# Strassen's method in the last feed-forward: seven block products in place of eight

## The chip, the cores and the metric

The kernel runs on one core of a Trainium2 chip. The metric is the device time of one execution in microseconds (us). It has five engines at work: TensorE multiplies matrices, ScalarE and VectorE do elementwise work and read TensorE's results from PSUM, GpSimd does elementwise work between tiles in SBUF, and SyncE (SP) issues the loads.

## The reference, cut to what matters

A two-layer backbone over 512 latent tokens (and 256 context tokens), width 1024, all in float32. Each layer has two feed-forwards around a token mixer. The last feed-forward of layer 1 works on the latents alone:

```python
def swiglu(h, w_in, w_out):
    gate, up = jnp.split(h @ w_in, 2, axis=-1)
    return (jax.nn.silu(gate) * up) @ w_out
...
x = x + 0.5 * m_lat[:, 8] * swiglu(modulate(rms_norm(x), m_lat[:, 6], m_lat[:, 7]), ffn_in[l, 1], ffn_out[l, 1])
...
return rms_norm(x, final_gain)
```

`w_in` is 1024 x 5632, `w_out` 2816 x 1024, so the two products take 512 x 1024 x 5632 and 512 x 2816 x 1024 multiplications.

## The kernel before

**Layout.** Activations lie feature-major: 8 tiles of 128 features x 512 tokens (`s.X`, `hs`). The 2816 hidden features are 22 row blocks of 128, worked in three parts of 8, 8 and 6 (`PARTS`, L30). A weight block of 128 x 128 is the stationary operand, 512 tokens are the moving one.

**Three matmuls for one product.** Every operand is split into a high part, rounded to fp32r, and the low rest: `split` (L114) makes the high part on ScalarE (L116) and the low part on VectorE (L117). `mm3` (L136) multiplies high by high, high by low and low by high (L138 to L140), all into one bank of PSUM.

**The stage.** `norm_mod` (L407) normalises the latents: for each of 8 feature tiles `modulate` writes x on VectorE (L403), the high part with the shift added on ScalarE (L404) and the low part on VectorE (L405). `ffn` (L422) then goes through a part's row blocks: for each one `weights` loads (L129) and splits four weight tiles of 128 x 512, and 2 x 8 x 3 matmuls fill one bank for gate and one for up. The gate takes a tanh on ScalarE (L466) and two VectorE operations with an operand in PSUM (L467, L468); the result is split into a `pL` tile. When a part is complete, each of the 8 output blocks is summed over the part's row blocks, and VectorE adds it, gated, to X (L487). In the last part ScalarE squares each new X block (L350), and GpSimd sums the squares (L354) for the final norm (`rms`, L356, then L1532).

**Order.** The stage has all 8 PSUM banks (`ps4`, pool d). The instruction order of each engine is laid out by the scheduler of the tile framework ahead of time; inside `merge` the order of TensorE is that of the program. Tiles with one tag share a fixed number of buffers, and a new one waits until the oldest is free: 4 raw weight tiles, 3 high and 3 low ones. The stage is called at the end of `run`, between the odd layer's output projection and the final norm.

Of the kernel before, what the change touches and what calls it, by code (L numbers as in the profile page):

```python
# [11 lines left out]
F32R = mybir.dt.float32r  # L12
I32 = mybir.dt.int32
AF = mybir.ActivationFunctionType
ALU = mybir.AluOpType
# [4 lines left out]
P = 128  # L20
D = 1024
KD = 8
NL = 512
# [5 lines left out]
NEG = -1e30  # L29
PARTS = ((0, 8), (8, 8), (16, 6))  # L30
LEVELS = (2, 4, 8, 16)


C_QG, C_KG, C_MU0, C_MU1 = 0, 1, 2, 17
# [8 lines left out]
def flat(x):  # L43
    return x.rearrange("p a t -> p (a t)")
# [26 lines left out]
class Kernel:  # L71
# [32 lines left out]
    def pair(self, s, tag, dtype=F32R):  # L104

        if tag == "hC":
            if not self.spare:
                x = self.t(self.ap, [P, 2, 2, s.T], tag, dtype)
                self.spare = [(x[:, i, 0], x[:, i, 1]) for i in (1, 0)]
            return self.spare.pop()  # L110
        x = self.t(self.ap, [P, 2, s.T], tag, dtype)
        return x[:, 0], x[:, 1]
# [32 lines left out]
    def go(self, gen):  # L145
        try:
            while True:
                next(gen)
        except StopIteration as e:
            return e.value  # L150
# [245 lines left out]
    def modulate(self, s, l, i, k, r, out):  # L396

        nc, m = self.nc, self.mods[l, s]
        shift, scale = m[:, i, k : k + 1], m[:, i + 1, k : k + 1]
        if k % 2 == 0:  # L400
            s.x = self.pair(s, s.g, F32)
        x = s.x[k % 2]
        nc.vector.scalar_tensor_tensor(x, s.X[k], scale, r, op0=ALU.mult, op1=ALU.mult)  # L403
        nc.scalar.activation(out[0], x, AF.Identity, bias=shift)  # L404
        nc.vector.scalar_tensor_tensor(out[1], x, shift, out[0].bitcast(F32), op0=ALU.add, op1=ALU.subtract)  # L405
# [16 lines left out]
    def ffn(self, l, f, streams, hs=None, bg=(0, 0), into=None):  # L422

        nc, aps = self.nc, self.aps
        i0 = 0 if f == 0 else 6
        start = hs is not None
        if hs is None:
            hs = {}
            for s in streams:
                hs[s] = yield from self.norm_mod(s, l, i0)  # L430
        win, wout = aps["ffn_in"][l, f], aps["ffn_out"][l, f]
        alone = len(streams) == 1
        ws = streams[0]
        for m0, part in PARTS:
            G = {s: [] for s in streams}
            for mi in range(part):
                pt = {}
                for s in streams:
                    if s is self.L:
                        pt[s] = (self.bank_of(s), self.bank_of(s))  # L440
                    else:
                        b = self.bank_of(s)
                        pt[s] = (b[:, :256], b[:, 256:])
                w = {}

                if streams == (self.L,):
                    order = [(g, k, streams) for k, g in itertools.product((0, 4), (0, 1))]
                elif start and not m0 + mi:
                    order = [(0, 0, streams), (1, 0, streams[:1]), (0, 4, streams), (1, 0, streams[1:]), (1, 4, streams)]
                else:  # L450
                    order = [(g, k, streams) for g, k in itertools.product((0, 1), (0, 4))]
                for g, k0, ss in order:
                    if ss[0] is ws:
                        w[g, k0] = self.weights(win[m0 + mi][:, g * 1024 + k0 * P :], 512, ws)
                    for k in range(k0, k0 + 4):
                        for s in ss:
                            while len(hs[s]) <= k:
                                yield None
                            self.mm3(pt[s][g], w[g, k0][k % 4], *hs[s][k], k == 0, k == KD - 1)
                        if k % 4 == 3 or k % 2 and alone:  # L460
                            self.background(bg[0])
                            yield sum(s.T for s in ss) / 400 * (1 if alone else 2), 0
                for s in streams:
                    pg, pu = pt[s]
                    a = self.t(self.fp, [P, NL], "fL", bufs=1 if s.lock else 2) if s is self.L else self.small("x", 4)
                    nc.scalar.activation(a, pg, AF.Tanh, scale=0.5)  # L466
                    nc.vector.scalar_tensor_tensor(a, a, 1.0, pg, op0=ALU.add, op1=ALU.mult)  # L467
                    nc.vector.tensor_tensor(a, a, pu, op=ALU.mult)  # L468
                    G[s].append(self.pair(s, s.g))
                    self.split(a, *G[s][mi])  # L470
                if alone:
                    yield from self.rest()
            last = m0 + part == NM

            for ss in [(s,) for s in streams[::-1]] if last else [streams]:
                X = {s: s.X for s in ss}
                if last and into and self.L in ss:
                    self.L.X = yield from into()
                for d in range(KD):
                    w = self.weights(wout[d][:, m0 * P : (m0 + part) * P], part * P, ws)  # L480
                    for s in ss:
                        po = self.bank_of(s)[:, : s.T]
                        for mi in range(part):
                            self.mm3(po, w[mi], *G[s][mi], mi == 0, mi == part - 1)
                        yield s.T * part / 800, 0
                        gate = self.mods[l, s][:, i0 + 2, d : d + 1]
                        nc.vector.scalar_tensor_tensor(s.X[d], po, gate, X[s][d], op0=ALU.mult, op1=ALU.add)  # L487
                        if last:
                            self.square(s, d, nc.gpsimd)
                    self.background(bg[1])  # L490
                    if alone:
                        yield from self.rest()
                if last:
                    ss[0].done.add((l, f))


    def project(self, src, hs, s, use, wait=False):
# [823 lines left out]
    def run(self):  # L1321
        nc, tc, aps, stop = self.nc, self.tc, self.aps, self.stop
        L, C, go = self.L, self.C, self.go
        with ExitStack() as ctx:
            def pool(n, **k):
                return tc.tile_pool(name=n, reuse_waits="tile", **k)
# [32 lines left out]
            with pool("ps", bufs=1, space=PSUM) as self.ps, pool("fp", bufs=1) as self.fp:  # L1359
# [18 lines left out]
                hs = {L: [], C: []}  # L1378
# [145 lines left out]
            with pool("ps4", bufs=1, space=PSUM) as self.ps, pool("fp3", bufs=1) as self.fp:  # L1524
                self.banks = dict(d=8)
                L.use(self.wp, self.tp, "d", acc)
                go(self.w_out(aps["odd_out"], L.o, L, 1, slice(4, 8)))
                go(self.ffn(1, 1, (L,)))
                r, _ = go(self.rms(L))
                for k in range(KD):  # L1530
                    x = L.X[k]
                    nc.vector.scalar_tensor_tensor(x, x, self.par[:, C_FG + k : C_FG + k + 1], r, op0=ALU.mult, op1=ALU.mult)  # L1532
                    nc.sync.dma_start(aps["out"][k * P : (k + 1) * P], x)
# [75 lines left out]
```

## Time and profile before

| what | us |
|---|---|
| median of three timed runs | 3230.58 (3228.81 to 3232.74) |
| the profiled execution | 3231.14 |
| its span, first to last instruction | 3229.4 |
| the stage's first matmul starts | 2852.41 |
| its last matmul starts | 3213.42 |
| mean granted TensorE clock | 0.981 |

The span is the time on which the profile's shares are based; the rest of the profiled execution lies around it. A row of the timeline gives start, duration, engine, line, operation, the tiles written and read, and shapes. Rows of one line can overlap, above all on TensorE, where the next matmul starts before the last one has drained; its cost in a dense stream is the distance between two starts. A row that ends in brackets tells how long the engine had been idle and what ended that.

### The profile page before, as it was taken

To read this page: it belongs to the slowest core of one execution; us is meant where nothing else is said; L and a number is where in the kernel's file an instruction comes from. 1 tells how busy PE (TensorE), PEld (TensorE's weight loads), DVE (VectorE), ACT (ScalarE), POOL (GpSimd) and SP (SyncE) were. 2 spreads that over 40 slices of the span, in tenths; PEclk is the share of its full clock that TensorE was granted. 3 is DMA by queue.
4 is the path that set the end of the run, shared out by engine and by line. 5 is a ranking of instruction groups with operands and counts; after the bars stand their busy time and mean duration, and the time that the engine had idled before them with its cause. 6 is when DMAs were issued, how large, how long until landed. Compare 5 with 4: busy or idle time off the path is not lost. (4 is left out here: it accounts for less than half of the span.)

```text
span 3229.4 us, 57800 instructions
## 1 busy us (share of the span) xinstructions
PE 3065.0 (95%) x22910; PEld 2619.3 (81%) x22910; DVE 2012.3 (62%) x3956; ACT 1246.7 (39%) x2595; POOL 309.8 (10%) x333
## 2 busy tenths in 40 slices
PE   5999999988999899998999999999999988999998
PEld 3888888886777788887888888888888877778887
DVE  7999983675667677777766434454444667744434
ACT  4222212444444444444444323343233556632322
POOL 3000000112232110102101000010000132010001
PEclk8999999999999899999999999999999999999999
DMA  6666671531112023332344333333333320023332
GB/s 225 208 212 216 215 259 59 167 105 49 43 46 80 23 87 98 97 97 71 99 141 138 105 97 96 96 116 98 95 98 93 110 74 24 27 83 97 98 97 87
DMA packets 174431, 349.59 MB, mean 108 GB/s; under 512 B 19408, under 2 KB 30544, under 8 KB 173776
## 3 DMA queue, kind: packets, MB, share of 16 engines
q1 hardware_dynamic: 169984, 340.86, 34.1%
q10 hardware_dynamic: 4176, 5.05, 0.5%
q8 instruction: 179, 2.93, 0.4%
q14 instruction: 92, 0.75, 0.1%
HBM read 340.59 MB, written 5.24 MB: 107 GB/s over the span
## 5 line engine op out<-in xcount | busy, mean ns | idle before, releaser
L116 ACT ACTIVATE whi<-raw 128x512 fp32r<-128x512 f32 (+1 forms) x996 | 615.5, 619 | 1364.5 <-PE d L139 498.6
L117 DVE TENSOR_TENSOR wlo<-raw,whi 128x512 fp32r<-128x512 f32 (+1 forms) x996 | 682.9, 688 | 685.4 <-ACT whi L116 671.9
L138 PE MATMUL d<-hL,whi 128*128 128x512 f32 x944 | 381.8, 405 | 3.9 <-ACT hL L404 3.9
L139 PE MATMUL d<-hL,whi 128*128 128x512 f32 x944 | 375.6, 398 | 1.8 <-DVE hL L405 1.8
L140 PE MATMUL d<-hL,wlo 128*128 128x512 f32 x944 | 373.2, 396 | 1.8 <-DVE wlo L117 1.8
L138 PE MATMUL d<-hC,whi 128*128 128x256 f32 x968 | 297.8, 308 | 7.4 <-ACT whi L116 4.3
L140 PE MATMUL d<-hC,wlo 128*128 128x256 f32 x968 | 278.1, 287 | 11.4 <-DVE wlo L117 11.4
L284 DVE SCALAR_TENSOR_TENSOR junk<-qL,cb 128x1024 bf16<-128x1024 f32 x224 | 273.4, 1221 | 12.2 <-DMA qL<-wmod 9.6
L139 PE MATMUL d<-hC,whi 128*128 128x256 f32 x968 | 276.9, 286 | 0.0
L140 PEld LDWEIGHTS d<-hL,wlo 128*128 128x128 f32 x944 | 180.4, 191 | 43.7 <-DVE wlo L117 3.1
L138 PEld LDWEIGHTS d<-hC,whi 128*128 128x128 f32 x968 | 188.1, 194 | 22.0 <-issue 7.5
L138 PEld LDWEIGHTS d<-hL,whi 128*128 128x128 f32 x944 | 180.8, 192 | 28.0 <-ACT hL L404 5.6
L139 PEld LDWEIGHTS d<-hL,whi 128*128 128x128 f32 x944 | 180.9, 192 | 23.8 <-DVE hL L405 3.1
L140 PEld LDWEIGHTS d<-hC,wlo 128*128 128x128 f32 x968 | 188.4, 195 | 14.0 <-DVE wlo L117 13.7
L139 PEld LDWEIGHTS d<-hC,whi 128*128 128x128 f32 x968 | 188.6, 195 | 0.5
L138 PE MATMUL d<-pL,whi 128*128 128x512 f32 x416 | 162.8, 391 | 0.0
L140 PE MATMUL d<-pL,wlo 128*128 128x512 f32 x416 | 162.2, 390 | 0.6 <-DVE wlo L117 0.6
L139 PE MATMUL d<-pL,whi 128*128 128x512 f32 x416 | 162.2, 390 | 0.0
L138 PE MATMUL g<-hL,whi 128*128 128x512 f32 x384 | 149.4, 389 | 0.0
L139 PE MATMUL g<-hL,whi 128*128 128x512 f32 x384 | 149.4, 389 | 0.0
L140 PE MATMUL g<-hL,wlo 128*128 128x512 f32 x384 | 149.4, 389 | 0.0
L354 POOL TENSOR_TENSOR acc<-acc,sq 128x512 f32<-128x512 f32 x30 | 38.9, 1297 | 925.9 <-issue 708.4
(533 smaller groups left out, 6596.5 us busy)
## 6 DMA issues: line engine op xcount, KB each, us to landing
raw<-ffn_in SPq DMA_DIRECT2D x528, 256.0 KB, 2.9
qL<-wmod SPq DMA_DIRECT2D x132, 512.0 KB, 4.2
raw<-ffn_out SPq DMA_DIRECT2D x248, 256.0 KB, 2.7
raw<-even_in SPq DMA_DIRECT2D x84, 256.0 KB, 2.6
raw<-even_out SPq DMA_DIRECT2D x32, 256.0 KB, 2.6
raw<-odd_in SPq DMA_DIRECT2D x32, 256.0 KB, 2.8
raw<-ffn_out SPq DMA_DIRECT2D x56, 128.0 KB, 2.1
pL<-wmod SPq DMA_DIRECT2D x8, 512.0 KB, 8.7
```

The lines of the kernel that those rows point to most:

```text
L116: self.nc.scalar.activation(hi, src, AF.Copy)
L117: (eng or self.nc.vector).tensor_tensor(lo, src, hi.bitcast(F32), op=ALU.subtract)
L138: mm(out, w[0], mh, start=first, stop=False)
L139: mm(out, w[0], ml, start=False, stop=False)
L140: mm(out, w[1], mh, start=False, stop=last)
L284: nc.vector.scalar_tensor_tensor(self.t(self.fp, [P, D], "junk", bf), w, 0.5, self.cb[:, v], op0=ALU.mult, op1=ALU.mult, accum_out=out)
L354: eng.tensor_tensor(s.sq[0], s.sq[0], x, op=ALU.add)
```

## The change

The last feed-forward is computed by `ffn7` in place of `ffn`. A product of 2 x 2 blocks is formed from seven products of block sums (Strassen's method in Winograd's form) and not from eight products. The 2 x 2 blocks are: for the weights, gate and up rows (or two output blocks) by the two halves of the features summed over; for the activations, the two halves of the features by the two halves of the tokens, so that each matmul has 256 moving columns.

- `forms` makes, from a pair of activation tiles, the four block sums T1 to T4 on GpSimd (256 columns each) and splits them, beside the blocks that are used as they are. For the normed input this is done four times, on `xs` (the x of `modulate`, to which ScalarE adds the shift in place); for the gated blocks, once for each pair of row blocks.
- `seven` loads four weight blocks, makes S1 to S4 on GpSimd, splits the seven left operands (the low part of S4 on GpSimd, the others on VectorE), runs the seven products into four PSUM banks, and combines them into `z` in SBUF: three VectorE sums that read PSUM, two ScalarE copies and one GpSimd sum.
- Row blocks 0 and 4 are still computed in the old way (`whole`), while the first `forms` run. The first row block of the next part is computed before the outputs of a part.

```diff
-                go(self.ffn(1, 1, (L,)))
+                self.merge(self.ffn7(1, 1))
@@ modulate
             s.x = self.pair(s, s.g, F32)
+            s.xs = s.xs if k else []
         x = s.x[k % 2]
+        s.xs.append(x)
@@
+SUMS, RAWS = 3, 1
...
+    def forms(self, b1, b2, tiles, plain=None):
+        nc = self.nc
+        if plain is None:
+            ba, bb = tiles[1:]
+            self.split(b1[:, :256], *ba)
+            self.split(b2, *bb)
+        else:
+            ba, bb = plain
+        a, b = slice(0, 256), slice(256, 512)
+        two = lambda x, c: (x[0][:, c], x[1][:, c])
+        F = dict(B11=two(ba, a), B21=two(bb, a), B22=two(bb, b))
+        t13, t24 = (self.t(self.tp, [P, 512], "sq", bufs=2) for _ in (0, 1))
+        tt = nc.gpsimd.tensor_tensor
+        tt(t13[:, a], b1[:, b], b1[:, a], op=ALU.subtract)
+        tt(t24[:, a], b2[:, b], t13[:, a], op=ALU.add)
+        tt(t13[:, b], b1[:, b], b2[:, b], op=ALU.add)
+        tt(t24[:, b], b2[:, a], t24[:, a], op=ALU.subtract)
+        parts = [("T1", t13[:, a]), ("T3", t13[:, b]), ("T2", t24[:, a]), ("T4", t24[:, b])]
+        whole = [t13, t24]
+        for x in tiles[0]:
+            if x[0].shape[1] == 512:
+                self.split(whole.pop(0), *x)
+                for c in (a, b):
+                    F[parts.pop(0)[0]] = two(x, c)
+            else:
+                name, y = parts.pop(0)
+                self.split(y, *x)
+                F[name] = x
+        return F
+    def seven(self, srcs, n, F, plain_first=False):
+        nc, K = self.nc, n // P
+        add, sub = ALU.add, ALU.subtract
+        w = {}
+        for name, src in zip(("A11", "A22", "A21", "A12"), srcs):
+            tag = next(self.raws)
+            x = w[name] = self.t(self.ap if tag == "aC" else self.fp, [P, 512], tag, bufs=RAWS)[:, :n]
+            nc.sync.dma_start(x, src)
+        for name, x, y in (("S3", "A21", "A11"), ("S1", "A21", "A22"), ("S2", "A22", "S3"), ("S4", "A12", "S2")):
+            w[name] = self.t(self.fp, [P, 512], "sum", bufs=SUMS)[:, :n]
+            nc.gpsimd.tensor_tensor(w[name], w[x], w[y], op=sub)
+        one, b57, b26, b34 = (self.bank() for _ in range(4))
+        two = lambda x: x.rearrange("p (a t) -> p a t", a=2)
+        out = dict(P1=one[:, :256], P5=b57[:, :256], P7=b57[:, 256:], P2=b26[:, :256], P6=b26[:, 256:], P3=b34[:, :256], P4=b34[:, 256:])
+        z = self.t(self.ap, [P, 4, 256], "xC")
+        order = [("P1", "A11", "B11"), ("P4", "A22", "T4"), ("P7", "S3", "T3"), ("P5", "S1", "T1"), ("P2", "A12", "B21"), ("P6", "S2", "T2"),
+                 ("P3", "S4", "B22")]
+        if plain_first:
+            order = [order[i] for i in (0, 4, 6, 5, 3, 2, 1)]
+        done = set()
+        for o, a, b in order:
+            tags = next(self.splits)
+            hi, lo = (self.t(self.wp, [P, 512], t, F32R, bufs=4 if t == "raw" else 3)[:, :n] for t in tags)
+            self.split(w[a], hi, lo, nc.gpsimd if a == "S4" else None)
+            for k in range(K):
+                c = slice(k * P, (k + 1) * P)
+                self.mm3(out[o], (hi[:, c], lo[:, c]), *F[k][b], not k, k == K - 1)
+            yield 0.35 * K
+            done.add(o)
+            if o == "P1":
+                p1 = self.small("sw", 2, self.tp)
+                nc.scalar.activation(p1, out[o], AF.Copy)
+            if o == "P5":
+                p5 = self.small("x", 4, self.tp)
+                nc.scalar.activation(p5, out[o], AF.Copy)
+            if o in ("P2", "P6") and done >= {"P2", "P6"}:
+                nc.vector.tensor_tensor(z[:, 0:4:3], two(b26), p1.unsqueeze(1).to_broadcast([P, 2, 256]), op=add)
+            if "u" not in done and done >= {"P2", "P6", "P5", "P7"}:
+                done.add("u")
+                u = self.t(self.fp, [P, 2, 256], "u", bufs=1)
+                nc.vector.tensor_tensor(u, two(b57), z[:, 3:4].to_broadcast([P, 2, 256]), op=add)
+                nc.gpsimd.tensor_tensor(z[:, 3], u[:, 1], p5, op=add)
+        nc.vector.tensor_tensor(z[:, 1:3], two(b34), u, op=add)
+        return z
+    def ffn7(self, l, f):
+        nc, aps, s = self.nc, self.aps, self.L
+        tt, stt = nc.vector.tensor_tensor, nc.vector.scalar_tensor_tensor
+        i0 = 0 if f == 0 else 6
+        hs = yield from self.norm_mod(s, l, i0)
+        xs = s.xs
+        win, wout = aps["ffn_in"][l, f], aps["ffn_out"][l, f]
+        both = lambda x: (x[:, 0], x[:, 1])
+        self.raws = itertools.cycle(["aC"] * 4 + ["A"] * RAWS)
+        self.splits = itertools.cycle([("whi", "wlo")] * 3 + [("raw", "raw")] * 2)
+        G = {}
+        def gated(g, u, mi, then):
+            a = self.t(self.fp, [P, NL], "fL", bufs=3)
+            nc.scalar.activation(a, g, AF.Tanh, scale=0.5)
+            stt(a, a, 1.0, g, op0=ALU.add, op1=ALU.mult)
+            tt(a, a, u, op=ALU.mult)
+            then(mi, a)
+        def whole(mi, then):
+            pg, pu = self.bank(), self.bank()
+            for k0, (g, pt) in itertools.product((0, 4), enumerate((pg, pu))):
+                w = self.weights(win[mi][:, g * 1024 + k0 * P :], 512, s)
+                for k in range(k0, k0 + 4):
+                    self.mm3(pt, w[k % 4], *hs[k], k == 0, k == KD - 1)
+                yield 2.7
+            gated(pg, pu, mi, then)
+        def chunk(m0, h):
+            def then(mi, a):
+                G[mi] = a
+                if mi >= m0 + h:
+                    pair = lambda: both(self.t(self.ap, [P, 2, 512], "pL", F32R))
+                    tiles = [[pair(), both(self.t(self.fp, [P, 2, 512], "t24", F32R, bufs=4))],
+                             both(self.t(self.fp, [P, 2, 256], "b11", F32R, bufs=4)), pair()]
+                    G[mi - h, mi] = self.forms(G.pop(mi - h), G.pop(mi), tiles)
+            return then
+        def inputs(m0, h, j):
+            mi = m0 + j // 2 + h * (j % 2)
+            z = yield from self.seven([win[mi][:, c : c + 512] for c in (0, 1536, 1024, 512)], 512, F)
+            z = flat(z)
+            gated(z[:, :512], z[:, 512:], mi, chunk(m0, h))
+        def outputs(m0, h, d, last):
+            srcs = [wout[d + i][:, (m0 + j * h) * P : (m0 + j * h + h) * P] for i, j in ((0, 0), (1, 1), (1, 0), (0, 1))]
+            z = yield from self.seven(srcs, h * P, [G[m0 + k, m0 + k + h] for k in range(h)], last and not d)
+            z = flat(z)
+            for i in (0, 1):
+                X = s.X[d + i]
+                stt(X, z[:, 512 * i : 512 * i + 512], self.mods[l, s][:, i0 + 2, d + i : d + i + 1], X, op0=ALU.mult, op1=ALU.add)
+                if last:
+                    self.square(s, d + i, nc.gpsimd)
+        m0, part = PARTS[0]
+        for mi in (0, part // 2):
+            yield from ((x, 0) for x in whole(mi, chunk(0, part // 2)))
+        F = []
+        for k in range(4):
+            for i in (k, k + 4):
+                nc.scalar.activation(xs[i], xs[i], AF.Identity, bias=self.mods[l, s][:, i0, i : i + 1])
+            tiles = [self.t(self.ap, [P, 2, n], tag, F32R) for tag, n in (("hC", 512), ("gC", 256), ("gC", 256))]
+            F.append(self.forms(xs[k], xs[k + 4], [[both(x) for x in tiles]], plain=(hs[k], hs[k + 4])))
+        todo = range(2, part)
+        for n, (m0, part) in enumerate(PARTS):
+            h, last = part // 2, n == len(PARTS) - 1
+            for j in todo:
+                yield from ((x, 0) for x in inputs(m0, h, j))
+            if not last:
+                m1, p1 = PARTS[n + 1]
+                yield from ((x, 0) for x in inputs(m1, p1 // 2, 0))
+                todo = range(1, p1)
+            for d in range(0, KD, 2):
+                yield from ((x, 0) for x in outputs(m0, h, d, last))
```

`split` takes the engine of the low part as its last argument; `mm3`, `bank` and `weights` are those of before.

## The prediction

> **What bounds the kernel now.** I read the page's busy shares first, then the windows over the stage that changes, then single matmuls.
>
> ```profile
> PE 3065.0 (95%) x22910; PEld 2619.3 (81%) x22910; DVE 2012.3 (62%) x3956; ACT 1246.7 (39%) x2595; POOL 309.8 (10%) x333
> ```
>
> PE is TensorE, DVE VectorE, ACT ScalarE, POOL GpSimd. TensorE is busy 95% of the 3229.4 us span. The stage in question is the last one. Columns of the windows: length, busy us and count of PE, weight loads, DVE, ACT, POOL, granted clock, DMA share, GB/s.
>
> ```profile
> 2873.00:2938.00 65.00, 65.00 (x288) 53.84 (x287) 27.94 (x42) 21.89 (x36) 0.00 (x0) 1.00 0.32 98
> 2938.00:2983.00 45.00, 45.00 (x200) 37.26 (x199) 17.57 (x26) 11.82 (x19) 0.00 (x0) 1.00 0.34 97
> ```
>
> The first is input products, the second output products. TensorE has no gap, VectorE is at 40%, ScalarE at 30%, GpSimd does nothing. So a cut in TensorE's work counts in full as long as the other engines keep up. What one matmul costs is read from starts, as the busy times overlap:
>
> ```profile
> 2900.17 0.39 PE L138 MATMUL d<-hL,whi 128*128 128x512 f32 x1
> ...
> 2901.98 0.39 PE L140 MATMUL d<-hL,wlo 128*128 128x512 f32 x1
> ```
> ```profile
> 1639.76 0.28 PE L140 MATMUL d<-gC,wlo 128*128 128x256 f32 x1
> ...
> 1641.20 0.28 PE L140 MATMUL d<-gC,wlo 128*128 128x256 f32 x1
> ```
>
> Eight steps lie between the first two starts: 0.2267 us for 512 columns. Twelve lie between the second two: 0.120 us for 256 columns, each with a weight load of its own.
>
> **What TensorE saves.** Before: 22 row blocks x 2 x 8 x 3 = 1056 input matmuls and 8 x 22 x 3 = 528 output matmuls, 1584 x 0.2267 = 359.0 us. After: two row blocks stay whole (96 x 0.2267 = 21.8). Twenty calls of `seven` make inputs, each 7 x 4 x 3 = 84 narrow matmuls (10.08 us, in place of 10.88). Twelve make outputs: eight of 84, four of 63 (7.56 us). That is 2604 x 0.120 = 312.5, with the whole ones 334.3. **TensorE alone saves 24.7 us.** Weights are loaded in the same number of bytes (four 256 KB loads per row block or pair of outputs, as now), so the SP queue gets no more work.
>
> **What the others must now do.** Durations:
>
> ```profile
> L117 DVE TENSOR_TENSOR wlo<-raw,whi 128x512 fp32r<-128x512 f32 x119 | 82.0, 689 | 131.7 <-ACT whi L116 131.7
> L116 ACT ACTIVATE whi<-raw 128x512 fp32r<-128x512 f32 x119 | 75.2, 632 | 212.6 <-PE d L139 210.3 <-PE d L140 2.4
> L468 DVE TENSOR_TENSOR fL<-fL,d 128x512 f32<-128x512 f32 x21 | 14.4, 687 | 21.2 <-PE d L140 21.2
> L466 ACT ACTIVATE fL<-d 128x512 f32<-128x512 f32 x21 | 12.2, 579 | 0.0
> L354 POOL TENSOR_TENSOR acc<-acc,sq 128x512 f32<-128x512 f32 x6 | 7.8, 1294 | 356.2 <-issue 342.2 <-ACT sq L350 14.0
> L116 ACT ACTIVATE whi<-raw 128x256 fp32r<-128x256 f32 x8 | 3.3, 418 | 9.7 <-PE d L139 9.7
> ```
>
> One `seven` for a row block needs, per 10.08 us of TensorE:
> - ScalarE: 7 splits x 0.63, copies of P1 and P5 (2 x 0.42), a tanh 0.58, half of the four splits in `forms` (1.16): 7.0 us. Covered.
> - VectorE: 6 splits x 0.69, three sums from PSUM x 0.69, two gate products x 0.69, half of `forms` (1.25): 8.8 us.
> - GpSimd: four sums of weight blocks and the low part of S4, 5 x 1.29, one 256-wide sum and half of four 256-wide ones in `forms` (0.74 each, next rows): 8.7 us.
>
> If these ran side by side, all would lie under TensorE. The trace shows that they don't:
>
> ```profile
> 2543.83 0.68 DVE L117 TENSOR_TENSOR wlo<-raw,whi 128x512 fp32r<-128x512 f32 x1
> 2544.43 0.47 DVE L403 SCALAR_TENSOR_TENSOR gC<-xC,mod1C,d 128x256 f32<-128x256 f32 x1
> 2544.82 1.13 DVE L405 SCALAR_TENSOR_TENSOR hC<-gC,mod1C,hC 128x256 fp32r<-128x256 f32 x1
> 2545.87 0.47 DVE L403 SCALAR_TENSOR_TENSOR gC<-xC,mod1C,d 128x256 f32<-128x256 f32 x1
> 2546.26 0.47 DVE L405 SCALAR_TENSOR_TENSOR hC<-gC,mod1C,hC 128x256 fp32r<-128x256 f32 x1
> ```
> ```profile
> 2544.33 1.33 POOL L354 TENSOR_TENSOR acc<-acc,sq 128x512 f32<-128x512 f32 x1 [3.41 <-ACT sq L350]
> ```
> ```profile
> 2609.73 2.25 DVE L117 TENSOR_TENSOR wlo<-raw,whi 128x512 fp32r<-128x512 f32 x2
> ```
> ```profile
> 2609.57 0.74 POOL L558 TENSOR_TENSOR sw<-sw,rope 128x256 f32<-128x256 f32 x1 [3.44 <-DVE sw L557]
> 2610.26 1.17 POOL L559 TENSOR_TENSOR x<-x,rope 128x256 f32<-128x256 f32 x1
> 2611.40 1.17 POOL L558 TENSOR_TENSOR sw<-sw,rope 128x256 f32<-128x256 f32 x1
> 2612.53 0.73 POOL L560 TENSOR_TENSOR x<-x,sw 128x256 f32<-128x256 f32 x1
> ```
>
> L405 has two inputs in SBUF and takes 0.47 us; under a GpSimd sum it takes 1.13 and ends 0.29 us after that sum (2545.95 against 2545.66). L403, with one input in PSUM (the tile d), keeps its 0.47 under the same sum. The other way round, the GpSimd sum ends 1.15 us after L117 does (2544.51). Two L117 and GpSimd's products alternate too: GpSimd's ends are 2610.31, 2611.43, 2612.57, so a 256-wide GpSimd operation and a 512-wide split take 1.13 us together, and the last ends 0.59 us after the split (2611.98). So **a VectorE operation with two SBUF inputs and a GpSimd operation run one after the other**; they hold what they share 0.55 us (VectorE, 512 wide; 0.275 for 256), 1.15 us (GpSimd, 512) and 0.59 us (GpSimd, 256).
>
> The Trainium skill, page "SBUF — State Buffer", section "SBUF: two separate sides", says the same against this change: VectorE with two SBUF inputs and GpSimd share a port pair, locked for the whole instruction. By whole instructions the sum below would be some 465 us in place of 388.6; the rows show shorter holds, and I keep the rows (rival 4).
>
> **The sum by turns.** Two SBUF inputs have the splits, the two gate products (in the new code gate and up stand in z, in SBUF, not in PSUM), the updates of X (from z too). The three sums into z and u read PSUM and don't count.
> - A call of `seven` with 512-wide weights: GpSimd 5 x 1.15 + 0.59 = 6.34, VectorE 8 x 0.55 = 4.40: 10.74 us. 28 of them (20 inputs, 8 outputs): 300.7.
> - Four with 384-wide weights: 5 x 0.86 + 0.59 + 6 x 0.41 + 2 x 0.55 = 8.45: 33.8, and six square sums on GpSimd x 1.15 = 6.9.
> - `forms` for 11 pairs: GpSimd 4 x 0.59, VectorE 3 x 0.55 + 0.275: 4.29 us, 47.2.
>
> 388.6 us in all, where TensorE needs 312.5. Per input call with its `forms` it is 12.9 us against 10.08 now needed and 10.88 before. The two whole row blocks stay at 21.8: the stage's start takes 8 modulations, 8 weight splits and the first `forms` (four times 0.55 + 2 x 0.275), 13.2 us of VectorE's turns, and 16 x 0.59 = 9.4 of GpSimd's, 22.6, just about TensorE's time. So the stage is 21.8 + 388.6 = 410.4, **51 us more than 359.0**.
>
> Unknown is how well the turns are filled. VectorE's PSUM sums, 32 x 3 x 0.69 = 66 us, either lie under GpSimd's turns (nothing) or in a row with everything (66). GpSimd needs 59% of an input call (7.5 of 12.9 us), and while VectorE sums from PSUM it mostly has a block sum waiting: I take a quarter, **17 us**. Both ends stay in the range.
>
> The end of the stage:
>
> ```profile
> 3209.77 0.75 DVE L487 SCALAR_TENSOR_TENSOR qL<-d,mod1L,qL 128x512 f32<-128x512 f32 x1 [0.66 <-PE d L140]
> 3213.85 0.75 DVE L487 SCALAR_TENSOR_TENSOR qL<-d,mod1L,qL 128x512 f32<-128x512 f32 x1 [3.33 <-PE d L140]
> ```
> ```profile
> 3210.61 0.63 ACT L350 ACTIVATE sq<-qL 128x512 f32<-128x512 f32 x1 [1.97 <-DVE qL L487]
> 3214.69 0.63 ACT L350 ACTIVATE sq<-qL 128x512 f32<-128x512 f32 x1 [3.45 <-DVE qL L487]
> ```
>
> Now the last product is followed by one update and one square, 1.4 us, and the sum of the block before ran earlier. After the change both last blocks come out of one sum: 0.69 + 0.75 + 0.63 + 1.29 = 3.4 us, **2 us more**. The product that S4 enters is the last of each call, and its low part is made on GpSimd behind the chain A21-A11, A22-S3, A12-S2; that wait has GpSimd's later sums queued behind it, but it is part of the turns above.
>
> 51 + 17 + 2 = 70. The profiled execution took 3231.1 us (its span 3229.4), 0.6 over the median of the three timed runs: **3301 us**, of which the unfilled turns make 3284 to 3350.
>
> **Rivals.**
> 1. *TensorE stays the bound* (the other side). For it: VectorE at 8.8 and GpSimd at 8.7 us fit under 10.08, and the calls can be worked ahead of TensorE. It needs GpSimd's hold to be short: the place is the block sums in `seven`, 155 of 512 width (28 x 5, and 4 x 5 x 0.75). The turns cost nothing against before once they fall by 51 us, that is when a GpSimd sum holds 0.82 us rather than 1.15 beside VectorE; below 0.66 TensorE is the bound. Then the stage is 334 and the time 3231 - 25 + 2 + some 4 for the start = 3212. Against it: every row above in which the two meet.
> 2. *GpSimd's order stalls TensorE.* If on GpSimd the sum into z[3] stands ahead of S4's low part, TensorE waits after its sixth product for two VectorE sums, that sum and the low part: 0.69 + 0.69 + 0.74 + 1.29 = 3.4 us, and behind them the next call's block sums wait too. A call is then at least 13.5 us: 28 x 13.5 + 4 x 11.0 + 21.8 = 444, so 3318 at least; with turns that no longer fill (the full 66) 3350, which I take. For it: GpSimd works in order. Against it: on VectorE the order follows readiness:
>
> ```profile
> 2909.21 0.69 DVE L468 TENSOR_TENSOR fL<-fL,d 128x512 f32<-128x512 f32 x1 [0.99 <-PE d L140]
> 2909.81 0.69 DVE L117 TENSOR_TENSOR wlo<-raw,whi 128x512 fp32r<-128x512 f32 x1
> 2910.59 0.69 DVE L117 TENSOR_TENSOR pL<-fL,pL 128x512 fp32r<-128x512 f32 x1
> ```
>
>    The split of the next row block's weights runs before that of the gated block, which the program has first.
>
> 3. *Half hidden.* If gate products and `forms` fall where GpSimd has nothing to do and cost no turns (20 x 1.1 + 47 = 69 us less), 70 - 69 leaves 1 us: 3225 to 3238. Against it: GpSimd has work in 59% of an input call.
> 4. *Turns as long as the instructions.* Then a 512-wide GpSimd sum holds 1.29 and a split 0.69 us: 28 x 12.7 + 4 x 10.5 + 7.7 + 11 x 5.45 = 465 us, 3361 with the 2 at the end. Against it: the pair of 0.74 and 0.69 took 1.13, not 1.43.
>
> **How the numbers follow.** The forecast gets 0.65, rival 1 0.10, rival 2 0.15, rival 3 0.05, rival 4 0.05. 0.2% is 6.5 us, about what a measurement of this kernel can tell. Faster 0.11 (rival 1 and the low edge of rival 3), same 0.04, slower 0.85. The range runs 3255 to 3362: the likeliest case with turns filled better than I think, and rivals 2 and 4; rivals 1 and 3 and a few hundredths above lie outside, about 0.18.
>
> **What would show it.** In the stage's windows VectorE's and GpSimd's busy times would add up to more than the window, TensorE falling to about 75-80%. L117 splits would rise from 0.69 to over 1 us, GpSimd's 512-wide sums above 1.3. The waits ahead of the new matmuls would name VectorE's low parts. Narrow matmuls would still start 0.120 us apart within a product. Wrong it would be if splits keep 0.69 us under GpSimd's sums: then rival 1 holds; if TensorE's gaps all stand ahead of the seventh product, rival 2.

## The result

| | us | beside before |
|---|---|---|
| before, median of 4 runs (3228.81 to 3234.52) | 3231.66 | |
| after, median of 4 runs (3334.39 to 3340.99) | 3338.51 | ratio 1.0332, 95% interval 1.0319 to 1.0345 |
| predicted | 3301 (3255 to 3362) | |

The change costs 107 us where the forecast said 70. Direction and range hold; the size is a third too small. Before's median here is 1 us above that of the prediction's runs.

Stage means here, in every kernel: from the start of its first matmul to the end of its last product. It took 361.2 us before (2852.4 to 3213.6) and 456.75 after (2858.75 to 3315.5). "Before" and "after" name the two kernels, before and after the change.

The page of after, its list of engines (busy us, share of the span, instructions):

```profile
PE 3088.0 (93%) x24026; PEld 2684.8 (80%) x24026; DVE 2256.2 (68%) x4150; ACT 1335.1 (40%) x2797; POOL 636.0 (19%) x585
```

GpSimd's busy time doubled. The shares of the whole span hide how different the stage is; the windows show it. These are the stage's phases in after, cut at the matmuls with which they begin: the whole blocks, the inputs of the first part with one block of the second (7 calls), the outputs of the first part (4 calls), 8 input calls, 4 output calls, 5 input calls, the last outputs; the last row is what comes behind the last product.

```profile
2858.75:2883.58 24.83, 24.28 (x97) 19.28 (x97) 18.04 (x27) 16.35 (x28) 2.46 (x2) 0.91 0.10 35
2883.58:2999.03 115.45, 84.06 (x602) 78.84 (x600) 89.74 (x98) 48.17 (x95) 85.93 (x71) 0.87 0.19 62
2999.03:3048.63 49.60, 44.43 (x325) 43.58 (x326) 49.33 (x49) 21.12 (x40) 36.32 (x26) 0.90 0.29 89
3048.63:3157.62 108.99, 92.60 (x686) 88.49 (x684) 95.47 (x100) 46.42 (x91) 82.96 (x63) 0.94 0.24 77
3157.62:3208.29 50.67, 44.56 (x325) 43.71 (x326) 50.30 (x50) 21.86 (x42) 36.43 (x26) 0.90 0.29 87
3208.29:3272.20 63.91, 54.69 (x423) 52.56 (x422) 55.90 (x60) 27.93 (x55) 47.78 (x38) 0.97 0.22 70
3272.20:3315.50 43.30, 34.57 (x253) 32.83 (x251) 39.25 (x48) 19.90 (x43) 33.11 (x28) 0.88 0.17 46
3315.50:3337.10 21.60, 5.76 (x25) 5.27 (x24) 8.80 (x13) 2.41 (x5) 6.32 (x5) 0.62 0.26 97
```

In the fourth row VectorE's 95.5 us and GpSimd's 83.0 make 178 us in a window of 109: two engines that wait for each other inside their instructions are both counted as busy. TensorE's 92.6 is not work either: its 672 matmuls at 0.120 us need 80.6. The groups of after within the stage (busy us, mean ns of one, idle before and what ended it) show where the time went in:

```profile
L118 DVE TENSOR_TENSOR wlo<-sum,whi 128x512 fp32r<-128x512 f32 x51 | 54.8, 1075 | 0.0
L118 DVE TENSOR_TENSOR wlo<-aC,whi 128x512 fp32r<-128x512 f32 x33 | 40.8, 1249 | 3.8 <-ACT whi L117 3.3
L599 DVE TENSOR_TENSOR fL<-fL,xC 128x512 f32<-128x512 f32 x20 | 31.7, 1584 | 2.5 <-POOL xC L578 0.6
L635 DVE SCALAR_TENSOR_TENSOR qL<-xC,mod1L,qL 128x512 f32<-128x512 f32 x24 | 29.9, 1278 | 1.5 <-POOL xC L578 1.3
L573 DVE TENSOR_TENSOR xC<-d,sw 128x512 f32<-128x512 f32 x32 | 21.7, 679 | 0.2 <-PE d L141 0.2
L546 POOL TENSOR_TENSOR sum<-aC,sum 128x512 f32<-128x512 f32 x44 | 62.4, 1418 | 60.7 <-issue 30.7 <-DVE wlo L118 18.4 <-DVE raw L118 6.3
```

The low part of a split (L118) rose from 0.69 us to 1.08 and 1.25. The gate's last product (L599), which read PSUM before, takes 1.58 us with both inputs in SBUF. The sum that reads PSUM (L573) takes 0.68 us, in the same stretch and beside the same GpSimd work. GpSimd's block sums (L546) take 1.42 where one alone took 1.29. What separates long from short on VectorE is where the inputs lie.

What TensorE waited for, added up over the steady part of the stage (2910 to 3270; us in total, times, longest):

```profile
PE d L139 <- ACT whi L117: 15.8, 8, 2.0
PE d L141 <- DVE wlo L118: 11.4, 17, 2.5
PE d L141 <- POOL raw L118: 8.3, 7, 1.6
PE d L141 <- POOL wlo L118: 7.9, 9, 1.7
PE d L141 <- DVE raw L118: 5.9, 8, 2.8
```

The low parts of S4 from GpSimd make 16.2 us of these 49.3, VectorE's low parts 17.3, and ScalarE's high parts 15.8. No single operand starves TensorE; all the supply is late.

The eight waits for ScalarE all have one shape, and it is no block sum that is missing there. One of them:

```profile
2939.78 0.63 ACT L117 ACTIVATE pL<-sq 128x512 fp32r<-128x512 f32 x1 [3.52 <-POOL sq L518]
...
2941.27 0.62 ACT L117 ACTIVATE whi<-aC 128x512 fp32r<-128x512 f32 x1
...
2941.94 0.58 PE L139 MATMUL d<-gC,whi 128*128 128x256 f32 x1 [1.97 <-ACT whi L117]
```

TensorE waits for the high part of a block that is loaded and needs no sum (aC). ScalarE has stood idle for 3.5 us, since the splits of a gated pair are ahead of it in its order, and these wait for GpSimd's sums in `forms` (L518). No run changes ScalarE's order, so what it is worth is open.

### The profile page after: what moved, and what is told of

Read it like the earlier page. It is cut to its first block, busy times and chain, and to the rows that moved or that the text cites. A ratio compares the mean times of both kernels' runs of the same rounds, so it can differ in the third digit from the quotient of the medians.

```text
span 3337.1 us, 60933 instructions
## 1 busy us (share of the span) xinstructions
PE 3088.0 (93%) x24026; PEld 2684.8 (80%) x24026; DVE 2256.2 (68%) x4150; ACT 1335.1 (40%) x2797; POOL 636.0 (19%) x585
## 5 line engine op out<-in xcount | busy, mean ns | idle before, releaser
L117 ACT ACTIVATE whi<-raw 128x512 fp32r<-128x512 f32 (+1 forms) x868 | 536.0, 619 | 1137.9 <-PE g L140 415.4
L118 DVE TENSOR_TENSOR wlo<-raw,whi 128x512 fp32r<-128x512 f32 (+1 forms) x868 | 596.6, 690 | 540.5 <-ACT whi L117 526.6
L139 PE MATMUL d<-hC,whi 128*128 128x256 f32 x1060 | 326.7, 308 | 8.1 <-ACT whi L117 4.4
L141 PE MATMUL d<-hL,wlo 128*128 128x512 f32 (+1 forms) x772 | 292.2, 379 | 15.0 <-DVE wlo L118 7.6
L140 PE MATMUL d<-hC,whi 128*128 128x256 f32 x1060 | 305.2, 288 | 0.0
L139 PE MATMUL d<-hL,whi 128*128 128x512 f32 (+1 forms) x772 | 300.2, 389 | 2.4 <-ACT hL L407 2.4
L140 PE MATMUL d<-hL,whi 128*128 128x512 f32 (+1 forms) x772 | 293.2, 380 | 2.7 <-DVE hL L408 2.6
L139 PEld LDWEIGHTS d<-hC,whi 128*128 128x128 f32 x1060 | 208.5, 197 | 23.1 <-issue 8.5
L140 PEld LDWEIGHTS d<-hC,whi 128*128 128x128 f32 x1060 | 208.9, 197 | 0.5
L141 PEld LDWEIGHTS d<-hL,wlo 128*128 128x128 f32 x772 | 148.6, 192 | 47.8 <-DVE wlo L118 10.8
L139 PE MATMUL d<-gC,whi 128*128 128x256 f32 x452 | 135.4, 299 | 31.6 <-ACT gC L117 17.7
L139 PEld LDWEIGHTS d<-hL,whi 128*128 128x128 f32 x772 | 149.1, 193 | 13.9 <-ACT hL L407 3.1
L140 PEld LDWEIGHTS d<-hL,whi 128*128 128x128 f32 x772 | 149.4, 194 | 12.4 <-DVE hL L408 4.3
L139 PE MATMUL d<-pL,whi 128*128 128x512 f32 (+1 forms) x350 | 128.2, 366 | 6.9 <-ACT pL L117 6.1
L140 PE MATMUL d<-gC,whi 128*128 128x256 f32 x452 | 131.7, 291 | 2.1 <-DVE gC L118 1.7
```

The source lines that it names most:

```text
L117: self.nc.scalar.activation(hi, src, AF.Copy)
L118: (eng or self.nc.vector).tensor_tensor(lo, src, hi.bitcast(F32), op=ALU.subtract)
L139: mm(out, w[0], mh, start=first, stop=False)
L140: mm(out, w[0], ml, start=False, stop=False)
L141: mm(out, w[1], mh, start=False, stop=last)
```

## The experiments

The theory: VectorE's operations with two SBUF inputs and GpSimd's sums take turns, and the sum of the turns exceeds TensorE's work. Against it stood that GpSimd or VectorE is simply too busy, that GpSimd's order stalls TensorE, and that the turns cost less or more than priced.

**e1: the turns by themselves.** A kernel that holds nothing but sums of tiles 512 or 256 wide, in stages one after the other:

```python
for _ in range(dve):
    vec(v, gate, x[1], op=add)                        # VectorE, both inputs in SBUF
for _ in range(psum):
    vec(v, ps, gate, op=add)                          # VectorE, one input in PSUM
for _ in range(gp):
    pool(g[:, :gpw], gate[:, :gpw], x[2][:, :gpw], op=add)
for _ in range(mem):
    nc.gpsimd.memset(g, 0.5)
```

> Eight stages of nothing but sums of 128x512 float32 tiles, one after the other; nothing of the reference is computed. Stage 1: 12 VectorE sums of two SBUF tiles. Stage 2: 12 GpSimd sums. Stage 3: both at once. Stage 4: 16 VectorE with 8 GpSimd. Stage 5: 16 VectorE sums with one operand in PSUM, with 12 GpSimd sums. Stage 6: as 3, GpSimd 256 wide. Stage 7: 12 GpSimd memsets. Stage 8: these with 12 VectorE sums. Theory of turns: stage 3 takes 12 x (0.55 + 1.15) = 20.4 us, stage 6 12 x 1.14 = 13.7 us, stage 5 only GpSimd's own 12 x 1.26 = 15.1 us, and the PSUM sums keep their 0.68 us. No turns: stage 3 takes 15.1 us, stage 6 8.4 us. Stage 8 tells whether a GpSimd operation that reads nothing takes turns too: open.

The timeline rows of two of its stages (start, us, engine, line): 12 sums of VectorE beside 12 of GpSimd, 512 wide (both) and with GpSimd's 256 wide (half).

```profile
35.87 19.03 DVE L32 TENSOR_TENSOR bothv<-gpo,t 128x512 f32<-128x512 f32 x12
35.92 20.10 POOL L36 TENSOR_TENSOR bothg<-gpo,t 128x512 f32<-128x512 f32 x12 [0.81 <-DVE gpo L46]
...
93.59 13.65 POOL L36 TENSOR_TENSOR halfg<-psgpo,t 128x256 f32<-128x256 f32 x12 [0.81 <-DVE psgpo L44]
```

A pair of 512-wide sums takes 20.10/12 = 1.675 us, against 0.55 + 1.15 = 1.70 as the prediction read it from single rows; the narrow pair 13.65/12 = 1.14, against 0.55 + 0.59. The groups of the same kernel show the two counter-tests, a VectorE sum that reads PSUM beside GpSimd sums, and GpSimd memsets:

```profile
L32 DVE TENSOR_TENSOR bothv<-gpo,t 128x512 f32<-128x512 f32 x12 | 18.6, 1554 | 0.4
L34 DVE TENSOR_TENSOR psgpv<-t,bot2o 128x512 f32<-128x512 f32 x16 | 11.1, 691 | 0.5
L36 POOL TENSOR_TENSOR psgpg<-bot2o,t 128x512 f32<-128x512 f32 x12 | 15.2, 1263 | 7.4 <-DVE bot2o L44 6.5
L38 POOL MEMSET memg<- 128x512 f32 x12 | 6.3, 525 | 0.0
L32 DVE TENSOR_TENSOR dvev<-t,t 128x512 f32<-128x512 f32 x12 | 8.3, 691 | 0.4
```

With an input in PSUM both engines keep their own time (691 and 1263 ns). The memsets of 525 ns ran beside the VectorE sums of the last row, which kept 691 ns (ten of its twelve lay beside memsets): here a GpSimd operation that reads nothing took no turn. The scheduler had moved some memsets and VectorE sums to other stages, so that the stage with GpSimd sums alone was not alone; it gives no number.

**e2: S4's low part on VectorE.**

```diff
-            self.split(w[a], hi, lo, nc.gpsimd if a == "S4" else None)
+            self.split(w[a], hi, lo)
```

> The low part of S4 goes from GpSimd to VectorE, 32 operations. Turns: each costs 0.55 where it cost 1.15, 28 x 0.60 + 4 x 0.45 = 19 us less, 3320. VectorE's own load is the bound, not the turns: 32 x 0.69 = 22 us more, 3360.

3321.66 us, ratio 1.0278 (1.0261 to 1.0295): 17 us off the change, nearly what the turns give. VectorE, already at 88% of the steady windows, got 32 more splits, and the kernel became faster; a bound by VectorE's own load would have made it slower.

**e3: all of GpSimd's share on VectorE,** the sums of squares excepted: e2's edit, and

```diff
-        tt = nc.gpsimd.tensor_tensor
+        tt = nc.vector.tensor_tensor
...
-            nc.gpsimd.tensor_tensor(w[name], w[x], w[y], op=sub)
+            nc.vector.tensor_tensor(w[name], w[x], w[y], op=sub)
...
-                nc.gpsimd.tensor_tensor(z[:, 3], u[:, 1], p5, op=add)
+                nc.vector.tensor_tensor(z[:, 3], u[:, 1], p5, op=add)
```

> All that the new stage does on GpSimd goes to VectorE, but for the squares at the end. Turns: nothing is left to take turns with; an input call is 16 VectorE operations x 0.60 + 0.35 and 1.75 of forms, 11.7 us, an output call stays at TensorE's 10.08; 20 x 11.7 + 8 x 10.1 + 4 x 8.3 + 21.8 = 370, with some 20 us lost at the start and end of the stage 3262. VectorE's load is the bound: an input call's 8.8 us grow to 13.5 of operation time, so slower than 3338, 3370 or more.

3278.84 us, ratio 1.0144 (1.0129 to 1.0159). One engine doing the work of two is 60 us faster than the two. Groups and a window of e3 (columns as above):

```profile
L118 DVE TENSOR_TENSOR wlo<-sum,whi 128x512 fp32r<-128x512 f32 x68 | 46.3, 689 | 3.7 <-ACT whi L117 3.7
L546 DVE TENSOR_TENSOR sum<-aC,sum 128x512 f32<-128x512 f32 x43 | 29.6, 688 | 0.1
```
```profile
3050.00:3100.00 50.00, 46.47 (x378) 45.50 (x378) 49.68 (x90) 27.61 (x53) 0.00 (x0) 1.00 0.29 95
```

The splits are back at 0.69 us, and a block sum costs 0.69 on VectorE where it held 1.15 us on GpSimd. VectorE, now alone, is busy 99% of that window and is the bound: 17 us more than expected. So e3 is a limit of its own, not TensorE's.

**e4: no block sums.** S1 to S4 are left out and the raw blocks stand in their place.

```diff
-            w[name] = self.t(self.fp, [P, 512], "sum", bufs=SUMS)[:, :n]
-            nc.gpsimd.tensor_tensor(w[name], w[x], w[y], op=sub)
+            w[name] = w[x]
```

> The four sums of weight blocks are left out: S1 to S4 are the blocks A21, A22, A12 themselves. All else stays. Turns: an input call falls to 1.15 + 0.59 + 4.4 + half of 4.29 = 8.3 us, under TensorE's 10.08; what is left over the 334 us of TensorE is the start (about 20) and the end: 3240 to 3250. If the waits came from the combination of the seven products instead (z, u, gates, forms), it stays above 3300.

3250.31 us in a single execution, 88 under the change. In the steady window TensorE is full:

```profile
2920.00:3000.00 80.00, 79.55 (x659) 78.96 (x658) 72.00 (x98) 44.74 (x89) 31.23 (x28) 1.00 0.31 97
```

659 narrow matmuls in 80 us are 0.121 us each. Even so the kernel stays 19 us behind before: the stage holds 334.2 us of matmuls and takes 372.1. At 0.120 us for a narrow matmul and 0.2267 for a wide one, the first 53.9 us of the stage (175 matmuls) lose 23 us and the last 43.2 (292 matmuls) lose 8; the 275 us between them lose 7. The two edges alone eat more than the 24.7 us that seven products save.

**e5: GpSimd as busy, without reading.** Each block sum becomes three memsets of the same tile (the sums are left out).

```diff
-            nc.gpsimd.tensor_tensor(w[name], w[x], w[y], op=sub)
+            for _ in range(3):
+                nc.gpsimd.memset(w[name], 0.5)
```

> Each of the four GpSimd sums of weight blocks becomes three GpSimd memsets of the same tile (3 x 0.46 = 1.4 us in place of 1.29): S1 to S4 hold a constant. GpSimd is as busy as before and in the same order, but reads nothing in them; run e1 has memsets and VectorE sums of two SBUF tiles side by side, each at its own pace. Turns: as with the sums left out, 3250, and the splits fall back to 0.69 us in most places. GpSimd's being busy, or its order, is what costs: 3330 or more.

3257.88 us in a single execution, 81 under the change. A group of e5 and its window:

```profile
L118 DVE TENSOR_TENSOR wlo<-sum,whi 128x512 fp32r<-128x512 f32 x51 | 41.0, 804 | 4.4 <-ACT whi L117 4.2
```
```profile
2920.00:3000.00 80.00, 77.78 (x640) 76.77 (x639) 69.67 (x95) 43.86 (x85) 72.50 (x119) 1.00 0.32 102
```

GpSimd is busy 91% of the window (74% in after from 2920 to 3000, 59.3 of 80), in the same order and with the same buffers, yet TensorE runs at 97%. So neither GpSimd's load nor its order is what slows the steady part. Between e4 and e5 lie 7.6 us, too little for single executions to rank. Both also lack the sums' waits for their inputs, and let go of loaded blocks earlier; that this is not the point rests on e3, which has the sums and their waits, though it meets a limit of its own.

**e6: the sums of the normed blocks first.** In the program the two whole row blocks stand ahead of the `forms` of the input; here they stand behind.

```diff
-        for mi in (0, part // 2):
-            yield from ((x, 0) for x in whole(mi, chunk(0, part // 2)))
         F = []
         for k in range(4):
...
             F.append(self.forms(xs[k], xs[k + 4], ...))
+        for mi in (0, part // 2):
+            yield from ((x, 0) for x in whole(mi, chunk(0, part // 2)))
```

It answers to a hole at the stage's start in after. The timeline there, ScalarE's shift of the last x blocks, GpSimd's operations and the matmul that waited:

```profile
2868.04 1.32 ACT L646 ACTIVATE pL<-pL,mod1L 128x512 f32<-128x512 f32 x2
...
2872.64 1.30 POOL L546 TENSOR_TENSOR sum<-aC,sum 128x512 f32<-128x512 f32 x1 [17.62 <-issue]
...
2884.61 1.04 POOL L517 TENSOR_TENSOR sq<-fL,sq 128x256 f32<-128x256 f32 x1 [9.52 <-DVE fL L599]
...
2889.32 1.10 POOL L516 TENSOR_TENSOR sq<-pL 128x256 f32<-128x256 f32 x1 [0.63 <-DVE pL L118]
...
2894.02 0.58 PE L139 MATMUL d<-gC,whi 128*128 128x256 f32 x1 [8.85 <-ACT gC L117]
```

All x blocks are ready at 2869.4. GpSimd starts on them (L516 on pL) 20 us later, because the first gated pair (L517 on fL) stands ahead, and its second half comes out of the second whole block and is ready only at 2884.6. TensorE then waits 8.85 us for the sums of x, and is short of them for longer:

```profile
2887.20:2911.10 23.90, 8.88 (x30) 6.94 (x31) 13.12 (x16) 8.77 (x18) 20.27 (x21) 0.50 0.04 12
```

GpSimd is busy for 20.3 of these 23.9 us, while TensorE starts 30 matmuls. So the input's `forms` did not run beside the two whole blocks, which had been kept whole for that.

> The sums and splits of the normed input (F) stand ahead of the two whole row blocks in the program, nothing else changes. In the profile after, GpSimd stands still 17.6 and 9.5 us at the start of the stage with a block sum and the sum for the first gated pair at the head of its queue, while these sums are ready behind them; TensorE then has about 20 us of gaps. If that order is the cause, 14 to 20 us less than the changed kernel: 3319 to 3325. If turns make the start slow, as the prediction had it, no more than 4 us less.

3321.58 us, ratio 1.0281 (1.0265 to 1.0297): 17 us off, as the order has it. The same two phases in e6:

```profile
2851.80:2882.10 30.30, 26.09 (x96) 18.95 (x97) 27.97 (x39) 21.43 (x40) 18.28 (x18) 0.91 0.05 19
2882.10:2976.80 94.70, 79.36 (x601) 75.65 (x599) 82.37 (x84) 40.95 (x81) 72.20 (x55) 0.96 0.25 78
```

The whole blocks lose 5.5 us under the sums that now run beside them, the seven input calls win 20.8.

**e7: e3 and e6 together.**

> As e3 (all on VectorE) with the order of e6. The start's gaps there are 13.5 us: 3266 to 3270 in place of 3279. The rest stays VectorE's: an input call of 11.7 us against 10.88 before, so still slower than before the change.

3273.06 us, ratio 1.0124 (1.0110 to 1.0138): 6 us better than e3, short of the 9 to 13 expected. Where VectorE is the bound, moving work to the start frees it of little.

**e8: a mixture.** If TensorE gains 0.8 us per call and VectorE lacks time, fewer calls should do. All sums on VectorE, `seven` in 9 of 22 input blocks and in the outputs of the first two parts, the rest as before the change:

```diff
+        def block(m0, h, j):
+            mi = m0 + j // 2 + h * (j % 2)
+            if m0 + j < 4 or j % 2 == 0:
+                yield from ((x, 0) for x in whole(mi, chunk(m0, h)))
+            else:
+                yield from ((x, 0) for x in inputs(m0, h, j))
```

> A version meant to beat both: all sums on VectorE, and the seven products only where VectorE has room: in half of the input blocks from the fifth on (9 of 22, so that a call's 11.7 us of VectorE are followed by a whole block's 6 in 10.88), and in the outputs of the first two parts; the last part's outputs in the old way. TensorE: 9 x 0.80 + 8 x 0.80 = 13.6 us less than before. An output call needs VectorE for 9.95 of 10.08 us, so some of it is lost: 3219 to 3230, 0.997 to 1.000.

3236.20 us, ratio 1.0015 (1.0006 to 1.0023): missed. The timeline of e8 shows one place where time is lost: SP's load of a whole block's weights, ScalarE's split and the matmul:

```profile
3069.50 2.21 SPq L130 DMA_DIRECT2D raw<-ffn_in  x4
...
3072.75 0.63 ACT L117 ACTIVATE whi<-raw 128x512 fp32r<-128x512 f32 x1 [5.65 <-DMA raw<-ffn_in]
...
3073.43 0.50 PE L139 MATMUL d<-hL,whi 128*128 128x512 f32 x1 [2.44 <-ACT whi L117]
```

The whole blocks load into the buffers named raw, which in the new kernel also hold split parts of `seven`. The load can only start when an earlier product has let go of them: over the stage SP's loads of whole blocks (L130) waited 34.4 us for matmuls in e8, and SP's loads waited for none in e9, which follows.

**e9: the mixture without that wait.** The whole blocks take their weights through the same rings of buffers as `seven`, and the input's `forms` are spread over the first blocks.

```diff
-                w = self.weights(win[mi][:, g * 1024 + k0 * P :], 512, s)
+                w = ring(win[mi][:, g * 1024 + k0 * P :], 512)
...
+                for k in (2 * j - 2, 2 * j - 1) if not m0 and j < 3 else ():
+                    F.append(self.forms(xs[k], xs[k + 4], ...))
```

> The mixture of e8 (all sums on VectorE; seven products in 9 of 22 input blocks and in the outputs of the first two parts, everything else as before the change), with two of the causes named for e8's miss taken out: the whole blocks take their weights through the same rings of loaded blocks and of high and low parts as the products, so that their loads no longer wait for a product to free one shared buffer, and the sums of the normalized blocks are spread over the first input blocks. If e8 missed because of those waits, the stage's matmul work of 345.5 us is left with about 5 us of gaps, so some 351 us against 361 before: 3220 to 3224 us, a ratio near 0.997. If VectorE's own load in the output calls (9.95 us of 10.08) or in the mixed blocks is what e8 missed by, it stays at 3232 us or above, a ratio of 1.000 or more.

3220.22 us against 3229.74 of before beside it, ratio 0.9973 (0.9962 to 0.9983): faster than both kernels, where expected. Its steady window and the whole stage:

```profile
2920.00:3000.00 80.00, 80.00 (x592) 76.60 (x591) 73.92 (x127) 40.13 (x73) 0.00 (x0) 1.00 0.34 104
...
2847.56:3197.70 350.14, 348.78 (x2196) 316.75 (x2197) 286.87 (x497) 172.48 (x310) 7.73 (x6) 0.99 0.29 92
```

TensorE has no gap while VectorE stands at 92%. The stage takes 350.1 us for 345.5 us of matmuls (1428 x 0.120 + 768 x 0.2267), 11 less than before. e9 changed two things at once, so how much the loads and how much the spread of `forms` gave is open, and with it what e8 missed by.

## Why the prediction was right, and where its size was off

**The mechanism held.** Slower, because VectorE's operations with two SBUF inputs and GpSimd's take turns: shown by e1 (the holds), e3 (no turns, 60 us back) and e5 (GpSimd busy without reading, 81 us back). Turns as long as the instructions (rival 4) would make the pair of e1 0.69 + 1.29 = 1.98 us; measured are 1.675, so rival 4 falls. The Trainium skill, page "SBUF — State Buffer", section "SBUF: two separate sides", names the same exclusion, but as a lock for the whole instruction, and the 1.675 us are shorter than that. The page also exempts GpSimd operations that read nothing, and e1's memsets agree (VectorE kept 691 ns).

**TensorE's work was sized right.** Narrow matmuls start 0.120 us apart at full clock (e4's window has 0.121), and the work is 334.2 us. The 24.7 us were never gained as time: even e4 does not show them.

**The sizes, term by term.** The prediction's sum by phases, with its 17 us of unfilled turns spread evenly over the 32 calls, beside the windows of after:

| phase | predicted | measured | off |
|---|---|---|---|
| two whole blocks | 21.8 | 24.8 | +3.0 |
| 20 input calls with all `forms` | 20 x 10.74 + 47.2 + 10.6 = 272.6 | 115.45 + 108.99 + 63.91 = 288.4 | +15.8 |
| 8 output calls | 8 x 10.74 + 4.3 = 90.2 | 49.60 + 50.67 = 100.3 | +10.1 |
| last four output calls | 33.8 + 6.9 + 2.1 = 42.8 | 43.3 | +0.5 |

- *The input calls* were sized about right in the steady state: 272.6/20 = 13.63 us, and the eight in the middle took 108.99/8 = 13.62. That this agrees to 0.01 us is luck: 0.53 us of a call is its share of the 17 us that were a guess, which no run measures by itself, and the last five took 63.91/5 = 12.78, 4.3 us less in all. The first seven took 115.45, 20.1 more than seven of 13.63. That is the hole at the start. **The step that failed** is the one on the start of the stage, which set 22.6 us of turns against 21.8 us of TensorE and concluded "just about TensorE's time". It counted turns and not the order on GpSimd, where the gated pair stood ahead of the sums of x. e6 changed that order alone and got 17 us back. It is the failure that rival 2 describes, GpSimd's order, at another place than rival 2 named.
- *The output calls* cost 12.5 us each and not 11.3. The timeline of after shows one mechanism: two updates of X (L635) stand on VectorE ahead of the low part for which TensorE waits.

```profile
3017.08 2.42 DVE L635 SCALAR_TENSOR_TENSOR qL<-xC,mod1L,qL 128x512 f32<-128x512 f32 x2
3019.43 0.68 DVE L118 TENSOR_TENSOR wlo<-sum,whi 128x512 fp32r<-128x512 f32 x1
...
3020.16 0.49 PE L141 MATMUL d<-t,wlo 128*128 128x256 f32 x1 [1.97 <-DVE wlo L118]
```

  Behind the gap the matmuls start about 0.21 us apart in place of 0.120, for 3.4 us at a granted clock of 0.50 (the windows of this gap stand at the end). No run took the updates away, so this reading is argued, not shown.
- *Rival 2 as named*, z[3] ahead of S4's low part, is not the main loss: S4's waits are 16.2 of 49.3 us, so the gaps don't all stand ahead of the seventh product, which was the sign given for it; and e2 freed 17 us, where the turns of that operation alone give 19. By the total alone rival 2, priced at 3350, would have been nearer to the measured 3338.5 than the forecast of 3301; it is the waits that speak against it.
- *The end of the stage* was priced at +2 and came to +5.8: behind the last product lay 15.8 us before and 21.6 after. In after the first sum of squares that had to wait starts at 3321.24, 5.7 us behind the last product, against 1.8 before (3215.37). The prediction took one combining sum for the last two blocks. The timeline of after shows three behind the last product (L573, L577, L579), since VectorE was still at the X updates of the call before:

```profile
3315.38 0.68 DVE L573 TENSOR_TENSOR xC<-d,sw 128x512 f32<-128x512 f32 x1
...
3316.42 0.69 DVE L577 TENSOR_TENSOR u<-d,xC 128x512 f32<-128x512 f32 x1 [0.37 <-ACT x L571]
3317.22 0.69 DVE L579 TENSOR_TENSOR xC<-d,u 128x512 f32<-128x512 f32 x1
...
3321.24 0.59 PE L369 MATMUL d<-ones,acc 128*128 128x1 f32 x2 [5.63 <-POOL acc L355]
```

  The rest is that the eight sums of squares ran at half clock, 3.62 us to the next step in place of 1.76.
- *Ahead of the stage* the profiled execution of after is 6.3 us later than that of before (2858.75 against 2852.41). The other runs, e1 aside, have the same code up to there and arrive between 2847.6 (e9) and 2856.2 (e5), so most of this part looks like scatter of single executions; whether the other executions of after are late there too, their times alone don't tell.

Phases (+29.4 against the predicted 427.4; before's own 361.2 against the 359.0 that the prediction took off gives 2.2 back), the end (+3.8) and the part ahead (+6.3) make up the 37.3 us by which the two spans (107.7 apart) differ beyond the forecast's 70.4 (51.4 + 17 + 2, rounded there to 70).

**Rival 1 and rival 3** fall with the splits at 1.08 to 1.25 us. What the prediction listed as signs came: VectorE and GpSimd busy for longer than the window together, splits above 1 us, GpSimd's sums above 1.3. The waits name VectorE's low parts for only 17.3 of the 49.3 us; ScalarE's place in the chain was not foreseen. TensorE was to fall to 75 to 80%; its work share in the eight steady input calls is 80.6/109.0 = 74%, while its busy column says 85%, since slow matmuls count as busy.

## What to carry to other kernels

Before work is moved to an idle engine, look in the trace for the two engines side by side with the same operands: if one of them stretches, add their times instead of comparing each with the bound. A saving on the bound engine is only worth what is left after the stage's edges, where the new operands have no cover; in e4, without block sums, the edges alone took back more than the 24.7 us. Use the method only as far as the helper engine has room: nine input blocks of 22 and two parts of the outputs, with VectorE alone, gained 0.27%.

## What the runs showed of the hardware

The prediction has no term for the granted clock, and in after the clock falls behind short gaps. Windows of after around one gap (the clock is the third column from the end):

```profile
3017.90:3020.20 2.30, 0.33 (x4) 0.13 (x2) 2.30 (x4) 0.63 (x1) 0.41 (x2) 1.00 0.25 92
3020.30:3023.70 3.40, 3.40 (x17) 3.40 (x18) 3.40 (x3) 0.63 (x1) 3.23 (x2) 0.50 0.19 45
```

An idle time of 1.97 us is followed by 3.4 us at 0.50. In the stage of after TensorE stood idle eleven times for 1.97 us at full clock, and ten of these were followed by such a stretch; of the eight idle times of 1.56 to 1.70 us none was. In e9 there is no such stretch between 2852.7 and 3200.9. The Trainium skill, page "TensorE: Matmul & The Clock Gate", Part 1, tells of windows of about 3.4 us and a half rate after an idle one; the length agrees, but the idle time here was shorter than a window. Steps from one matmul's start to the next that are too long by less than 0.3 us add up to some 32 us in after's stage, and 26 of them lie at half clock. Since the steady input calls took about what the turns give, these stretches seem to fall into time that TensorE had to spare; no run tried it.

The other surprise is that a 512-wide GpSimd operation that only writes cost VectorE nothing (525 ns, VectorE's sums still 691 ns, e1), while beside one that reads VectorE's sums took 1554 ns.
